# A two-layer trunk on one core: the last 16 tokens of the expert layer's first product by gathered rows, its dense part 240 columns wide

## The chip, the cores and the metric

The kernel runs on one core of a Trainium2 chip. The metric is the device time of one execution in microseconds (us), the median of several runs. Inside a core, TensorE (PE) multiplies matrices, VectorE (DVE), ScalarE (ACT) and GpSimd (POOL) work element by element, SyncE (SP) starts most of the transfers, and the DMA engines carry data between device memory and the core. Each engine works through its own list of instructions in order; they wait for one another by semaphores.

## What is computed

Two layers; each mixes tokens (`x + g1 * ...`) and then sends every token through a product-key retrieval over 16,384 one-neuron experts. With 256 tokens and a model width of 1024, the expert part is what the change touches:

```python
D_MODEL, SEQ, DEPTH = 1024, 256, 2
PEER_HEADS, PEER_TOPK, N_KEYS = 8, 16, 128

def peer_ffn(h, w_pq, sub_keys, expert_down, expert_up):
    ...
        q = (t @ w_pq).reshape(T, PEER_HEADS, 2, PEER_HALF)
        s = jnp.einsum('thpk,hpnk->thpn', q, sub_keys, preferred_element_type=jnp.float32)
        top_s, top_i = lax.top_k(s, PEER_TOPK)
        ...
        gate = jax.nn.softmax(best_s, axis=-1)
        u = expert_down[experts]
        act = jax.nn.gelu(jnp.einsum('td,thkd->thk', t, u, preferred_element_type=jnp.float32),
                          approximate=False)
        wgt = (gate * act).astype(t.dtype)
        vv = expert_up[experts]
        return jnp.einsum('thk,thkd->td', wgt, vv)

def hybrid_layer(x, c_act, ...):
    mod = (c_act @ w_ada + b_ada)[:, None, :]
    sh1, sc1, g1, sh2, sc2, g2 = jnp.split(mod, 6, axis=-1)
    h = rms_norm(x, norm1_g) * (1 + sc1) + sh1
    ...
    x = x + g1 * (merged @ w_out)
    h2 = rms_norm(x, norm2_g) * (1 + sc2) + sh2
    x = x + g2 * peer_ffn(h2, peer_wq, peer_sub_keys, peer_down, peer_up)
```

Every token picks 8 x 16 = 128 experts.

## The kernel before

A layer has these stages: a bridge that normalises the tokens, mixing (16 chunks of `w_in`, attention and its companions, 8 chunks of `w_out`), a second bridge, retrieval (16 chunks of `w_pq` and the two top-k searches, much of whose DVE work is put off as "fill"), the first product, the second product, and a closing combine.

**Weights.** A weight chunk is 128 x 1024 float32, 512 KB. SP loads it into one of seven `raw` buffers in the order of one long list (`seq`); ACT casts it to `hi` (L236), DVE takes the rest as `lo` (L229), each with three buffers. A chunk is then 24 matmuls in the one-pass type fp32r: for each of eight slices `d` of the model width hi times hi (L308), lo times hi (L309) and hi times lo (L310). The tokens `hh` are the moving operand, all 256 columns of them. Between weight chunks of `seq` stand "ada" chunks of `w_ada`: DVE multiplies one with the conditioning vector and sums it (L194) to get 128 entries of `mod`, needed by the next layer's bridges and gates. `mix` spreads them over a stretch of the list.

**First product.** The dense product of all tokens with all 128 chunks of `down` gives `ch`, 128 experts x 256 tokens per chunk; ACT applies the gelu. For the first `T` = 192 tokens the gates are spread over the expert grid by one-hot matrices: for each group of four tokens POOL compares an index row with `picks` four times (L925, f16), DVE compares (L928) and multiplies the result by the gates' two f16 parts (L930, twice 512 wide), and PE multiplies the two (L938, L939: eight f16 matmuls of 128 columns a group, 48 groups a layer). DVE multiplies gates and activations (L946 and the L97x lines). One-hots have two buffers (`R_ON`), so POOL and DVE build at most two groups ahead of PE. While fill work is left, `run_fill` works off a portion of it after every chunk; the gates start when the fill is empty. The last 64 tokens go another way: their activations are stored in device memory (`act_rows`), and the chosen ones, and the rows of `up`, are gathered by POOL with indirect DMAs (L1014, L1007).

**Second product.** 128 chunks of `up`, ten matmuls of 512 columns each (L1045), for the first 192 tokens; beside it DVE adds the gathered rows for the last 64 (L1041) by weights that L1032 to L1034 make. `R_ROWS` is where gathered rows land.

**What sets the order.** Each engine's list comes from a scheduler that simulates the program, except in the bridges and the combine, which are written out by hand. In the bridge DVE writes the normalised tokens slice by slice (L356, L428; ACT's part is L358), and PE follows with the first chunks' matmuls slice by slice (`second_pair`). The first two chunks of layer 1's `w_in` are used whole, in float32 (L388), and hold their `raw` buffers until then.

## Time and profile before

| | |
|---|---|
| median of 3 runs | 1744.12 us (1743.03 to 1744.75) |
| the profiled execution | 1742.29 us, of which the span is 1740.6 us |
| TensorE's granted clock, mean | 0.998 of full speed |

| stretch, us from the span's start | length | PE busy | DVE busy | POOL busy |
|---|---|---|---|---|
| first product, layer 0: 188.65 to 582.46 | 393.81 | 393.75 | 345.43 | 249.12 |
| second product, layer 0: 582.46 to 879.44 | 296.98 | 296.98 | 266.66 | 181.15 |
| first product, layer 1: 1039.40 to 1433.05 | 393.65 | 393.59 | 299.42 | 212.01 |
| second product, layer 1: 1433.05 to 1729.60 | 296.55 | 296.55 | 264.97 | 176.26 |

The busy time of an engine is the sum of its instructions' durations, overlaps counted once. PE's matmuls overlap: one of 287 ns starts some 119 ns after the one before. What counts for PE is therefore the distance between two starts.

### The profile page before, as it was taken

The numbers are of one execution on the slowest core, as the hardware profiler recorded it, in microseconds if no ns is written. First come the engines' busy times: TensorE is split into PE (matmuls) and PEld (weight loads), VectorE is DVE, ScalarE is ACT, GpSimd is POOL, SyncE is SP. The second block draws the span as 40 slices with busy tenths as digits, with TensorE's granted clock in tenths as the row PEclk, the third lists the DMA queues.
The fourth block names the chain that finished last, engine by engine and source line by source line (L and its number), as shares of the span: only waits on it lengthen the run. The fifth ranks groups of instructions, "written<-read, shape, count | busy, mean of one in ns | idle before, by whom it ended". The sixth has DMA issues, their size and how long they took to land.

```text
span 1740.6 us, 32293 instructions
## 1 busy us (share of the span) xinstructions
PE 1716.8 (99%) x11848; PEld 1573.4 (90%) x11848; DVE 1435.0 (82%) x2679; ACT 906.9 (52%) x1469; POOL 835.3 (48%) x697
## 2 busy tenths in 40 slices
PE   7999999999999999999999999999999999999998
PEld 6889999999999888888888999999999998888887
DVE  6858998888898799999966699957777768999996
ACT  2446455555444555555557555544544455555553
POOL 1000205588998477776100012236777737777630
PEclk9999999999999999999999999999999999999999
DMA  9965568887778799999843545676656668999993
GB/s 381 341 234 175 163 210 278 304 262 253 257 250 262 240 344 392 383 352 383 325 149 122 170 162 182 202 248 197 196 188 197 192 194 283 378 394 347 375 368 114
DMA packets 159281, 454.49 MB, mean 261 GB/s; under 512 B 50513, under 2 KB 50897, under 8 KB 157970
## 3 DMA queue, kind: packets, MB, share of 16 engines
q1 hardware_dynamic: 99936, 363.38, 60.3%
q0 software_dynamic: 23936, 80.50, 12.2%
q10 hardware_dynamic: 35250, 8.56, 2.2%
q8 instruction: 93, 1.52, 0.4%
q14 instruction: 66, 0.54, 0.1%
HBM read 440.75 MB, written 11.54 MB: 260 GB/s over the span
## 4 chain that ended last, share of the span: by engine, by line
PE 90%; DVE 7%; DMA 1%; ACT 1%; issue 0%; SPq 0%; DVEq 0%; ACTq 0%
PE acc L1045 34%; PE ch L308 15%; PE ch L309 14%; PE ch L310 14%; PE ch L306 3%; DVE lo L229 2%; PE g L938 1%; PE g L939 1%; PE ch L388 1%; DMA raw<-in_w_ada 1%; PE acc L308 1%; PE acc L310 1%; PE acc L309 1%; DVE arena L770 1%; DVE arena L771 1%; DVE arena L769 1%
## 5 line engine op out<-in xcount | busy, mean ns | idle before, releaser
L236 ACT CAST hi<-raw 128x1024 fp32r<-128x1024 f32 x554 | 582.0, 1051 | 624.0 <-PE ch L310 337.4
L229 DVE TENSOR_TENSOR lo<-raw,hi 128x1024 fp32r<-128x1024 f32 x554 | 675.6, 1224 | 179.8 <-ACT hi L236 169.1
L308 PE MATMUL ch<-hh,hi 128*128 128x256 f32 x2336 | 669.4, 287 | 0.0
L309 PE MATMUL ch<-hh,lo 128*128 128x256 f32 x2336 | 662.2, 284 | 0.1
L310 PE MATMUL ch<-hh,hi 128*128 128x256 f32 x2336 | 660.8, 283 | 0.0
L925 POOL TENSOR_SCALAR arena<-iota,picks 128x128 f16<-128x128 f16 x384 | 431.0, 1139 | 238.0 <-PE g L939 110.3
L309 PEld LDWEIGHTS ch<-hh,lo 128*128 128x128 f32 x2336 | 442.3, 189 | 0.7 <-DVE lo L229 0.5
L308 PEld LDWEIGHTS ch<-hh,hi 128*128 128x128 f32 x2336 | 442.1, 189 | 0.3 <-issue 0.3
L310 PEld LDWEIGHTS ch<-hh,hi 128*128 128x128 f32 x2336 | 442.2, 189 | 0.0
L1045 PE MATMUL acc<-hi,hh 128*128 128x512 f32 x1536 | 400.1, 395 | 0.0
L1045 PEld LDWEIGHTS acc<-hi,hh 128*128 128x128 f32 x1536 | 289.3, 188 | 67.3
L1045 PE MATMUL acc<-lo,hh 128*128 128x512 f32 x1024 | 280.9, 395 | 0.0
L1007 POOL DMA_INDIRECT arena<-in_up,arena x128 | 181.3, 1417 | 112.3 <-DVE arena L1041 77.5
L1045 PEld LDWEIGHTS acc<-lo,hh 128*128 128x128 f32 x1024 | 192.9, 188 | 44.9
L1014 POOL DMA_INDIRECT arena<-act_rows,arena x128 | 182.0, 1422 | 85.0 <-PE acc L1045 46.8
L1041 DVE SCALAR_TENSOR_TENSOR arena<-arena 128x1024 f32<-128x1024 f32 x126 | 162.1, 1286 | 0.0
L194 DVE SCALAR_TENSOR_TENSOR raw<-raw,arena 128x1024 f32<-128x1024 f32 x96 | 116.7, 1220 | 9.4 <-DMA raw<-in_w_ada 5.8
L930 DVE TENSOR_TENSOR arena<-arena,parts 128x512 f16<-128x512 f16 x192 | 77.0, 441 | 31.2 <-PE g L938 31.2
L784 POOL CAST arena<-arena 128x512 f16<-128x512 uint32 x32 | 29.2, 925 | 139.5 <-DVE arena L773 108.0
L748 POOL DMA_DIRECT2D arena<-in_keys x2 | 1.1, 562 | 170.2 <-issue 117.2
L949 ACT ACTIVATE arena<-g 128x344 f32<-128x344 f32 (+23 forms) x96 | 31.2, 325 | 73.6 <-DVE arena L946 72.5
L989 DVE TENSOR_TENSOR hh<-arena,hh 128x768 fp32r<-128x768 f32 (+1 forms) x66 | 61.6, 934 | 1.1 <-ACT hh L987 1.1
(232 smaller groups left out, 1610.1 us busy)
## 6 DMA issues: line engine op xcount, KB each, us to landing
raw<-in_down SPq DMA_DIRECT2D x256, 512.0 KB
raw<-in_up SPq DMA_DIRECT2D x256, 512.0 KB
raw<-in_w_ada SPq DMA_DIRECT2D x96, 512.0 KB
raw<-in_w_pq SPq DMA_DIRECT2D x32, 512.0 KB
raw<-in_w_in SPq DMA_DIRECT2D x26, 512.0 KB
raw<-in_w_out SPq DMA_DIRECT2D x16, 512.0 KB
act_rows<-ungated ACTq DMA_DIRECT2D x128, 64.0 KB
arena<-in_w_in SPq DMA_DIRECT2D x6, 512.0 KB
```

The costliest lines, as they stand in the source:

```text
L194: op = nc.vector.scalar_tensor_tensor(raw, raw, 1.0, cact, op0=OP.mult, op1=OP.mult, accum_out=mods[layer][:, col:col + 1])
L229: nc.vector.tensor_sub(lo, raw, hi.bitcast(F32))
L236: nc.scalar.copy(hi, raw)
L308: nc.tensor.matmul(dst, hi[:, cols], k[0], start=start, stop=False, **kw)
L309: nc.tensor.matmul(dst, lo[:, cols], k[0], start=False, stop=False, **kw)
L310: nc.tensor.matmul(dst, hi[:, cols], k[1], start=False, stop=stop, **kw)
L925: nc.gpsimd.tensor_scalar(oh[:, i, :], iota, picks[:, t:t + 1], None, op0=OP.is_equal)
L930: nc.vector.tensor_tensor(og[j], on, wide(1 + j), op=OP.mult)
L1007: nc.gpsimd.indirect_dma_start(out=R_ROWS[slots[k]], out_offset=None, in_=rows, in_offset=bass.IndirectOffsetOnAxis(ap=where_row[:, k:k + ...
L1014: nc.gpsimd.indirect_dma_start(out=R_ACTS[:, k % (2 * GROUP), :], out_offset=None, in_=act_rows[layer][:, :], in_offset=bass.IndirectOffse ...
L1041: nc.vector.scalar_tensor_tensor(R_SUM, v, w8[:, k:k + 1], R_SUM, op0=OP.mult, op1=OP.add)
L1045: nc.tensor.matmul(acc[piece], w, u[:, lo:hi], start=piece not in opened, stop=last, skip_group_check=True)
```

## The change

The first product's dense part takes the first `TD` = 240 tokens. For the last `TA` = 16 tokens the 128 chosen rows of `down` are gathered (`fetch_few`: POOL, 16 indirect DMAs of 128 rows a layer, four in flight in `R_ROWS`) and multiplied with the token's own input by DVE (`dot`, 16 of 128 x 1024 a layer). `own_inputs` prepares these inputs: 16 matmuls with the identity, two ACT copies, seven DMAs on SP's queue. `few_weights` makes gelu times gate of the sums and sends them to `w8a` by eight DMAs; `weights` adds them. `to_picks` sends eight more small DMAs. A new input, `down_rows`, is the table laid out by rows.

The gated one-hots of a group are made by one DVE operation, 1024 wide, where there were two of 512. For that, the two one-hots share a tile and interleave: `oh`, PE's stationary operand, was contiguous and now has a stride of two elements.

Sixteen ada chunks of layer 1 (groups 3 and 4) move in `seq` from layer 0's first product to layer 1's `w_in`. Two small regions change place.

```diff
+TA = 16
+TB = TS - TA
+TD = S - TA
+EIGHTHS = P // TA
+DOT_LAST = 104
...
-            body += tail
+            body = mix(body, ada(1, [3, 4]), 2) + tail
...
-            dn = mix(dn, ada(0, [5], "held") + ada(1, range(5), "held"), 24, 124)
+            dn = mix(dn, ada(0, [5], "held") + ada(1, range(3), "held"), 24, 124)
...
+                for e in range(EIGHTHS):
+                    nc.sync.dma_start(few[e * TA:(e + 1) * TA, :2], chosen[P - TA:, :, e * TA:(e + 1) * TA])
...
-                nc.gpsimd.tensor_scalar(oh[:, i, :], iota, picks[:, t:t + 1], None, op0=OP.is_equal)
...
-            for j in range(2):
-                nc.vector.tensor_tensor(og[j], on, wide(1 + j), op=OP.mult)
+                nc.gpsimd.tensor_scalar(oh[:, i // 2, :, i % 2], iota, picks[:, t:t + 1], None, op0=OP.is_equal)
...
+            nc.vector.tensor_tensor(gated, on[:, :, None].to_broadcast(shape), of[:, :, :, None].to_broadcast(shape),
+                                    op=OP.mult)
...
-                nc.tensor.matmul(dst, oh[:, i, :], og[0][:, i // 2, :, i % 2], start=True, stop=False)
-                nc.tensor.matmul(dst, oh[:, i, :], og[1][:, i // 2, :, i % 2], start=False, stop=True)
+                at = slice(None), i // 2, slice(None), i % 2
+                nc.tensor.matmul(dst, oh[at], og[0][at], start=True, stop=False)
+                nc.tensor.matmul(dst, oh[at], og[1][at], start=False, stop=True)
...
+        def own_inputs(pss):
+
+            for h, ps in enumerate(pss):
+                for c in range(4):
+                    dst = ps[:, c * P:(c + 1) * P]
+                    for k in range(2):
+                        nc.tensor.matmul(dst, hh[:, k, 4 * h + c, P:S], identr, start=k == 0, stop=k == 1)
+                nc.scalar.copy(own[P // 2:, h * 512:(h + 1) * 512], ps[P // 2:, :])
+            for e in range(EIGHTHS - 1):
+                nc.sync.dma_start(own[e * TA:(e + 1) * TA], own[P - TA:])
...
+        def fetch_few(k):
+            if k < TA:
+                nc.gpsimd.indirect_dma_start(
+                    out=R_ROWS[k % 4], out_offset=None, in_=rows_down,
+                    in_offset=bass.IndirectOffsetOnAxis(ap=few_row[:, k:k + 1].bitcast(U32), axis=0))
+
+        def dot(k):
+
+            v = R_ROWS[k % 4]
+            tc.keep_in_program_order(nc.vector.scalar_tensor_tensor(
+                v, v, 1.0, own, op0=OP.mult, op1=OP.mult, accum_out=few_w[:, k:k + 1]))
...
+                nc.vector.tensor_add(w, w, w8a[:, g * GROUP:(g + 1) * GROUP])
...
-            chunk_mm(ps[:, j * S:(j + 1) * S], next_chunk())
+            w = next_chunk()
+            for d in range(DC):
+                products(ps[:, j * TD:(j + 1) * TD], w, slice(d * P, (d + 1) * P),
+                         (hh[:, 0, d, :TD], hh[:, 1, d, :TD]), d == 0, d == DC - 1)
...
+            if start is not None and i == start + 2:
+                for k in range(4):
+                    fetch_few(k)
+            at = (start or 128) + 8
+            while at <= i and dotted < min(TA, -(-TA * (i + 1 - at) // (DOT_LAST - at))):
+                dot(dotted)
+                fetch_few(dotted + 4)
+                dotted += 1
+                if dotted == TA:
+                    few_weights()
```

The lines of the changed kernel are 10 to 50 higher than those before. Three places of the order follow.

POOL's list in layer 0's first product; L925 and L939 are the one-hots, L1007 fetches rows of `up`, L1043 rows of `down`. Before:

```order
L784 CAST arena<-arena 128x512 x16
L925 TENSOR_SCALAR arena<-iota,picks 128x128 x12
L1007 DMA arena<-in_up,arena 128x1024 x4
L925 TENSOR_SCALAR arena<-iota,picks 128x128 x180
L1014 DMA arena<-act_rows_102,arena 128x64 x16
```

After:

```order
L794 CAST arena<-arena 128x512 x16
L939 TENSOR_SCALAR arena<-iota,picks 128x128 x12
L1043 DMA arena<-in_down_rows,few 128x1024 x4
L939 TENSOR_SCALAR arena<-iota,picks 128x128 x20
L1043 DMA arena<-in_down_rows,few 128x1024
L939 TENSOR_SCALAR arena<-iota,picks 128x128 x4
L1043 DMA arena<-in_down_rows,few 128x1024
L939 TENSOR_SCALAR arena<-iota,picks 128x128 x8
```

The fetches of `up` rows that stood behind the first three groups have gone further down, and the fetches of `down` rows now stand singly between one-hots, every four to twelve of them; each but the first four waits for the dot that frees its rows.

DVE's list in layer 0's first product, some two thirds in: L229 and L239 are `lo`, L194 and L204 ada, L930 and L944 the gated one-hots, L928 and L941 the plain ones, L974/L946 and L991/L963 the use of the gates, L1050 a dot. Before:

```order
L194 SCALAR_TENSOR_TENSOR raw,mod_110<-raw,arena 128x1024
L928 TENSOR_TENSOR arena<-iota_87,parts 128x512 x2
L229 TENSOR_TENSOR lo<-raw,hi 128x1024
L974 TENSOR_TENSOR arena<-arena,gt 128x2x104
L930 TENSOR_TENSOR arena<-arena,parts 128x512 x2
L946 SCALAR_TENSOR_TENSOR arena<-arena,g 128x86x4
L229 TENSOR_TENSOR lo<-raw,hi 128x1024
L194 SCALAR_TENSOR_TENSOR raw,mod_110<-raw,arena 128x1024
L928 TENSOR_TENSOR arena<-iota_87,parts 128x512
```

After:

```order
L204 SCALAR_TENSOR_TENSOR raw,mod_114<-raw,arena 128x1024
L941 TENSOR_TENSOR arena<-iota_87,parts 128x2x256 x2
L239 TENSOR_TENSOR lo<-raw,hi 128x1024
L991 TENSOR_TENSOR arena<-arena,gt 128x2x104
L944 TENSOR_TENSOR arena<-arena,parts 128x1024
L963 SCALAR_TENSOR_TENSOR arena<-arena,g 128x86x4
L1050 SCALAR_TENSOR_TENSOR arena,few<-arena 128x1024
L239 TENSOR_TENSOR lo<-raw,hi 128x1024
L941 TENSOR_TENSOR arena<-iota_87,parts 128x2x256
```

Where an ada operation stood, every second or third time a dot stands now, and the pairs of L930 are single.

DVE's list in the bridge into layer 1: L340 and L350 update the tokens, L404 and L414 sum squares, L324 and L334 end the norm, L356/L428 and L366/L438 write the normalised slices that PE waits for. Before:

```order
L1107 COPY arena<-acc 128x512 x2
L340 SCALAR_TENSOR_TENSOR arena<-acc,mod_109,arena 128x256 x8
L229 TENSOR_TENSOR lo<-raw,hi 128x1024
L404 TENSOR_TENSOR arena<-arena 128x256 x3
L229 TENSOR_TENSOR lo<-raw,hi 128x1024
L404 TENSOR_TENSOR arena<-arena 128x256 x3
L324 RECIPROCAL rn<-rn 128x2
L356 SCALAR_TENSOR_TENSOR arena<-arena,mod_110,g 128x256 x2
L428 SCALAR_TENSOR_TENSOR hh<-arena,mod_110,hh 128x256
L356 SCALAR_TENSOR_TENSOR arena<-arena,mod_110,g 128x256
```

After:

```order
L350 SCALAR_TENSOR_TENSOR arena<-acc,mod_113,arena 128x256 x4
L414 TENSOR_TENSOR arena<-arena 128x256 x3
L204 SCALAR_TENSOR_TENSOR raw,mod_114<-raw,arena 128x1024
L239 TENSOR_TENSOR lo<-raw,hi 128x1024 x2
L414 TENSOR_TENSOR arena<-arena 128x256 x3
L204 SCALAR_TENSOR_TENSOR raw,mod_114<-raw,arena 128x1024
L334 RECIPROCAL rn<-rn 128x2
L366 SCALAR_TENSOR_TENSOR arena<-arena,mod_114,g 128x256 x2
L204 SCALAR_TENSOR_TENSOR raw,mod_114<-raw,arena 128x1024
L438 SCALAR_TENSOR_TENSOR hh<-arena,mod_114,hh 128x256
L366 SCALAR_TENSOR_TENSOR arena<-arena,mod_114,g 128x256
L438 SCALAR_TENSOR_TENSOR hh<-arena,mod_114,hh 128x256
```

Ada operations now stand in this bridge, nine of the sixteen ahead of its last slice; the sixth to the ninth stand behind the second group of sums, and three of those between the slices (after `L366 ... x2` and further on). The raw buffers of the seventh and eighth are those of the two whole chunks, which PE gives back after the last L388.

## Rows read from the trace of the kernel before

**Rows 1.** The page: busy time by engine, and the chain of work that ended last by engine and by line.

```profile
PE 1716.8 (99%) x11848; PEld 1573.4 (90%) x11848; DVE 1435.0 (82%) x2679; ACT 906.9 (52%) x1469; POOL 835.3 (48%) x697
...
PE 90%; DVE 7%; DMA 1%; ACT 1%; issue 0%; SPq 0%; DVEq 0%; ACTq 0%
PE acc L1045 34%; PE ch L308 15%; PE ch L309 14%; PE ch L310 14%; PE ch L306 3%; DVE lo L229 2%; PE g L938 1%; PE g L939 1%; PE ch L388 1%; DMA raw<-in_w_ada 1%; PE acc L308 1%; PE acc L310 1%; PE acc L309 1%; DVE arena L770 1%; DVE arena L771 1%; DVE arena L769 1%
```

**Rows 2.** The same chain in order of time, the two second products: start, length, what. A row is 1,278 records of 512 columns.

```profile
582.46 296.98 PE acc L1045 x1278
...
1433.05 296.52 PE acc L1045 x1276
```

**Rows 3.** Busy time by stretch, of the instructions on tile `ch` alone: 19 chunks of the fill part (the count has three records that reach in from outside); columns: stretch and length, PE, PEld, DVE, ACT, granted clock, DMA share, GB/s.

```profile
212.83:266.94 54.11, 54.11 (x459) 54.11 (x457) 0.00 (x0) 6.53 (x20) 1.00 0.66 205
```

**Rows 4.** PE in order of time in the gate part: a group's eight f16 matmuls of 128 columns, and fp32r matmuls behind it; start, duration.

```profile
453.11 0.22 PE L939 MATMUL g<-arena 128*128 128x128 f16 x1
...
453.45 0.22 PE L939 MATMUL g<-arena 128*128 128x128 f16 x1
...
453.92 0.29 PE L308 MATMUL ch<-hh,hi 128*128 128x256 f32 x1
...
455.12 0.29 PE L309 MATMUL ch<-hh,lo 128*128 128x256 f32 x1
```

**Rows 5.** The chain in order of time: float32 records of 128 columns (L628), and of 64 columns (L1116, the width is in rows 6).

```profile
83.50 0.89 PE g L628 x8
...
880.36 0.22 PE acc L1116 x2
```

**Rows 6.** PE in order of time: the operation of the last row above, whose records the timeline sets a little earlier than the chain.

```profile
880.20 0.39 PE L1116 MATMUL acc<-fold,arena 128*128 128x64 f32 x2
```

**Rows 7.** Groups of instructions by line: count, busy time, mean ns of one, idle time ahead and what ended it.

```profile
L925 POOL TENSOR_SCALAR arena<-iota,picks 128x128 f16<-128x128 f16 x384 | 431.0, 1139 | 238.0 <-PE g L939 110.3 <-DVE arena L838 52.5 <-DVE picks L855 52.0
L1007 POOL DMA_INDIRECT arena<-in_up,arena x128 | 181.3, 1417 | 112.3 <-DVE arena L1041 77.5 <-issue 14.2 <-DVE arena L1000 9.2
L1041 DVE SCALAR_TENSOR_TENSOR arena<-arena 128x1024 f32<-128x1024 f32 x126 | 162.1, 1286 | 0.0
L194 DVE SCALAR_TENSOR_TENSOR raw<-raw,arena 128x1024 f32<-128x1024 f32 x96 | 116.7, 1220 | 9.4 <-DMA raw<-in_w_ada 5.8 <-ACT arena L363 3.6
L930 DVE TENSOR_TENSOR arena<-arena,parts 128x512 f16<-128x512 f16 x192 | 77.0, 441 | 31.2 <-PE g L938 31.2
L938 PE MATMUL g<-arena 128*128 128x128 f16 x384 | 53.9, 222 | 0.0
L938 PEld LDWEIGHTS <-arena 128*128 128x128 f16 x384 | 35.2, 96 | 3.4
L308 PEld LDWEIGHTS ch<-hh,hi 128*128 128x128 f32 x2336 | 442.1, 189 | 0.3 <-issue 0.3
L824 DVE TENSOR_TENSOR arena<-arena,iota 128x2048 f16<-128x2048 f16 x8 | 9.7, 1212 | 0.0
L194 DVE DVE_READ_ACCUMULATOR raw<-raw,arena 128x1 f32 x96 | 8.1, 84 | 0.0
L336 ACT ACT_TABLE_LOAD x6 | 7.7, 1283 | 0.1
```

**Rows 8.** Busy time by stretch, all instructions: most of the fill part, then the gate part of layer 0 and of layer 1. Columns: length, PE, PEld, DVE, ACT, POOL, granted clock, DMA share, GB/s.

```profile
201.79:265.41 63.62, 63.62 (x539) 63.62 (x538) 63.59 (x241) 32.75 (x49) 5.12 (x5) 1.00 0.66 203
...
318.00:500.00 182.00, 182.00 (x1648) 180.77 (x1647) 156.12 (x280) 89.64 (x178) 156.31 (x133) 1.00 0.80 257
...
1170.00:1390.00 220.00, 220.00 (x1991) 218.52 (x1990) 160.76 (x281) 107.49 (x213) 164.94 (x164) 1.00 0.62 193
```

**Rows 9.** The bridge into layer 1, the chain in order of time: PE's last L388 and the norm's broadcast, then the first slice.

```profile
885.17 6.13 PE ch L388 x28
...
893.06 0.46 PE g L330 x4
893.55 0.49 DVE arena L356
894.06 0.52 ACT hh L358
```

**Rows 10.** DVE in order of time in the same bridge; idle time ahead in brackets.

```profile
882.25 0.69 DVE L1107 COPY arena<-acc 128x512 f32<-128x512 f32 x1 [2.78 <-PE acc L1045]
882.86 3.23 DVE L340 SCALAR_TENSOR_TENSOR arena<-acc,mod,arena 128x256 f32<-128x256 f32 x8
...
892.42 0.17 DVE L324 RECIPROCAL rn<-rn 128x2 f32<-128x2 f32 x1 [1.76 <-ACT rn L323]
893.55 0.87 DVE L356 SCALAR_TENSOR_TENSOR arena<-arena,mod,g 128x256 f32<-128x256 f32 x2 [0.96 <-PE g L330]
894.60 0.48 DVE L428 SCALAR_TENSOR_TENSOR hh<-arena,mod,hh 128x256 fp32r<-128x256 f32 x1 [0.18 <-ACT hh L358]
```

**Rows 11.** Busy time by stretch, columns as in rows 8: the bridge's end, layer 1's `w_in`, and ACT's fullest part of it.

```profile
888.00:896.00 8.00, 6.87 (x41) 5.93 (x39) 4.90 (x12) 3.79 (x10) 0.00 (x0) 1.00 0.70 223
900.00:945.00 45.00, 45.00 (x373) 43.99 (x373) 31.66 (x69) 32.65 (x76) 0.00 (x0) 1.00 0.43 141
928.00:936.00 8.00, 8.00 (x65) 7.58 (x64) 7.87 (x26) 7.32 (x31) 0.00 (x0) 1.00 0.41 132
```

More of the change, by code (lines that the diff above doesn't have):

```diff
@@ L57, in hybrid_trunk @@
 def hybrid_trunk(ctx: ExitStack, tc: tile.TileContext, x_in, c_in, vec_in, w_ada, w_in, w_out, w_pq,
-                 keys, down, up, rel_bias, sgu_w, sgu_b, out):
+                 keys, down, up, down_rows, rel_bias, sgu_w, sgu_b, out):
     nc = tc.nc
@@ L101, in hybrid_trunk @@
     c_dram = dram.tile([1, D], F32, name="c_dram")
-    act_rows = [dram.tile([P * P, TS], F32, name=f"act_rows{n}") for n in range(DEPTH)]
+    act_rows = [dram.tile([P * P, TB], F32, name=f"act_rows{n}") for n in range(DEPTH)]
     x_dram = dram.tile([P, DC * S], F32, name="x_dram")
@@ L143, in hybrid_trunk @@
     R_SUM = region(112 * S, D)
-    R_ACTS = region(116 * S, 2 * GROUP, TS)
-    R_IX = region(120 * S, 3, TS)
+    R_ACTS = region(116 * S, 2 * GROUP, TB)
+    own = region(120 * S, D)
     R_S = region(80 * S, 2, 16, P)
@@ L155, in hybrid_trunk @@
     R_SCR = region(116 * S, 2, 256)
+    chosen = region(108 * S, 2, P)
     R_PK = region(118 * S, 10, P)
@@ L991, in split @@
                     splits[i + k] = hi[:, k, :P], lo[:, k, :P], slot[:, k, T + P:2 * T + TS]
-        rows = up.rearrange("l j i c -> (l j i) c")
-        where_act, where_row, w8 = (R_IX[:, n, :] for n in range(3))
+        rows, rows_down = (w.rearrange("l j i c -> (l j i) c") for w in (up, down_rows))
+        where_act, where_row, w8, w8a = (index[:, n, :] for n in range(4))
+        few_at, few_gate, few_row, few_w = (few[:, n, :] for n in range(4))
         free = deque(range(4))
@@ L1134, in experts @@
         start = None
+        dotted = 0
         for i in range(128):
@@ L1152, in experts @@
                 start = i + 1
+                own_inputs([bank("acc", 4) for _ in range(2)])
                 make_onehots(0)
```

58 lines of the change are left out of this document (37 added, 21 removed).

## The prediction

> **What bounds the kernel now.** I read the shares of the page first: PE is busy for 99% of the span, and the chain that ended last runs over PE for 90% of it, mostly over the second product (L1045) and the first (L308 to L310) [rows 1]. So a change is worth what it takes from PE's list, as long as no other engine becomes late. The chain by time then shows both second products as one gapless piece each, 297 us [rows 2]; the change doesn't touch them. In the first product I read what one matmul takes. In the fill part 456 fp32r matmuls of 256 columns take 54.11 us, 118.7 ns each [rows 3]; in the gate part ten distances take 1.20 us, 120 ns each [rows 4]. Last, the stretches of the other engines: in the fill part DVE is busy for 63.59 of 63.62 us, in layer 0's gate part DVE and POOL both for 156 of 182 us, in layer 1's DVE for 161 and POOL for 165 of 220 us [rows 8]. There is little room in layer 0.
>
> **The narrower product.** It has 2 x 128 x 24 = 6144 matmuls. For the distance at 240 columns there is no row. From 256 to 512 columns it grows from 120 ns to 296.98/1278 = 232.4 ns [rows 2, 4], 0.44 ns a column, so 16 columns are worth 7.0 ns and 6144 matmuls 43.0 us. The upper bound is the shortest distance that any 4-byte record shows: 8 float32 records of 128 columns take 0.89 us, 111 ns each [rows 5], and with 64 columns it is no less, 0.22 us for two [rows 5, 6]. Half the columns and the same distance: there something else than the columns sets it, and loading weights is what they have in common. Down to 111.5 ns the gain is 8.5 ns a matmul, 52 us. The lower bound is nothing, if the distance at 256 columns is already set by weights. I take 43.0, by the slope, whose result of 113 ns lies just above the floor.
>
> The rows show that floor of 111 ns for 4-byte weights. The Trainium skill, "TensorE: Matmul & The Clock Gate", section "LDWEIGHTS (loading the stationary operand)", says that a load takes its column count over 1.2 ns, 107 ns for 128 columns, and the section "Back-to-back issue gap" gives a lone matmul N/2.4 + 2.5 ns, 109 ns for 256 columns. By these two the distance would go from 109 to 107 ns, an estimate of 2.5 ns or 15 us in place of 43. The traced 120 and 232 ns are 11 and 17 ns longer than that formula's, so I follow the slope; no run shown here has 240 columns.
>
> **Added to PE.** `own_inputs`: 32 matmuls of 128 columns at the floor's 111 ns, 3.6 us. They stand in bridges where PE partly waits for slices, so nothing to 3.6; I take 3.6.
>
> **The fill part.** DVE is full there now and makes 23 `lo` in 63.62 us, 2.77 us a chunk [rows 8]. PE would need 24 x 113 ns = 2.71 us. For some 25 chunks a layer DVE sets the pace: 2 x 25 x 0.06 = 3 us given back (0 to 5).
>
> **The gate part, layer 0.** Of the 182 us [rows 8], 1648 records less 266 f16 ones are fp32r: 1382 x 7.0 = 9.7 us go, leaving 172.3 us of PE. DVE: 33 groups lose two L930 of 441 ns and get one of 1024 columns; 441 ns for 512 and 1212 ns for 2048 [rows 7] give 0.70 us by interpolation, so -6.1 us. Of ada, 48 operations over the list's chunks 24 to 124 become 32, so 28 in these 58 chunks become some 19, of 1.22 + 0.08 us each: -12.1 us. Dots: 16 over the 70 chunks up to 104, 14 in this stretch, at L1041's 1286 + 84 ns, +19.2 us. DVE: 156.1 + 1.0 = 157.1 of 172.3 us, 91%: it fits. POOL gets 14 indirect DMAs at L1007's 1.417 us [rows 7], 156.3 + 19.8 = 176.1 us against 172.3. It doesn't fit, and every fetch but the first four waits on POOL's queue for a dot of DVE, with the next one-hots queued behind it and PE waiting for them two groups later. Now PE is ahead of POOL often enough: POOL waited 110 us for L939 [rows 7]. I take 3.8 us for the excess and about as much again for the waits: 8 us (0 to 16, the end where each of 16 fetches costs a DVE operation of a microsecond).
>
> **The gate part, layer 1.** POOL: 164.9 + 22.7 of 220 - 11.6 = 208.4 us, 90%, and DVE has room as well [rows 8]. Nothing, as long as POOL stays under PE.
>
> **Transfers.** The 16 gathered blocks a layer are as many bytes as 16 ada chunks, so layer 0's first product moves what it did, at a DMA share of 0.80 [rows 8]. SP's 23 small DMAs a layer stand between `raw` loads, each behind what it waits for; seven buffers hold 7 x 2.7 = 19 us of PE's work, so I cost them at nothing. A wait longer than that would reach PE with its excess.
>
> **The ada chunks moved.** They cost nothing in layer 0 and now sit in layer 1's bridge. Four come early, two of them around the copies and L340 on the path [rows 10], up to 2 x 1.3 us; two more hide before L324, where DVE idled 1.76 us and PE worked for 6.13 us on L388 [rows 9, 10]. The seventh to ninth stand between the slices for which PE waits: 3 x 1.3 = 3.9 us, straight on the path. The seventh's load also starts only after the last L388, at some 893 us; 0.52 MB at the 223 GB/s of that stretch [rows 11] is 2.4 us, where DVE would be there at 894.4 [rows 10], a wait of about 1 us. In `w_in` DVE has 31.66 of 45 us busy [rows 11] and gets seven more, 9 us: it fits, nearly. Two table loads of 1.28 us [rows 7] on ACT at 7.32 of 8 us [rows 11] and one more `hi` in the bridge: some 2 us. Together 9 us (3 to 14).
>
> **The sum.** 1742.3 (the profiled execution) - 43.0 + 3.6 + 3 + 8 + 9 = 1722.9 us. That execution lies 1.8 us below the median, so 1724.7, rounded 1725. With every cost at its upper bound it is 1740; with the floor and every cost at its lower bound 1695, but a PE that fast meets DVE and POOL sooner, so the forecast's own range ends at 1703.
>
> **The rivals.**
> *Strided weights, slower.* `oh` is loaded with a stride of two. Today eight f16 matmuls start 57 ns apart (0.34 us for six) [rows 4] and their loads are 96 ns records, against 189 for 4-byte weights [rows 7]: they load faster. If the stride ends that, 768 matmuls go from 58 to 111 ns, +41 us, and POOL's 8 us vanish behind it: 1758. It decides from about 83 ns on: 25 ns x 768 is the whole forecast gain. For it: the rate is visibly not the 4-byte one and nothing strided is in the trace. Against it: the operation stays f16 with 128 columns. The Trainium skill, same page, "Weight-path perf modes", says that the fast load takes packed or strided columns; by that, no cost, and no run here shows it.
> *Weights set the distance, slower.* If the 120 ns are the 111 of a 4-byte weight load and a fixed rest, 240 columns save nothing, DVE and POOL aren't pressed, and 3.6 + 9 us are added: 1744.1 + 12.6 = 1757. For it: 120 is near 111. Against it: the columns from 256 to 512 cost 0.44 ns each, so 256 lies on the slope or close to its foot. If the foot lies between 240 and 256 and a third of the gain is left, 14 us against 3.6 + 9 + 2, it is 1744, no change. The estimate of 15 us by the skill's two sections above would come out there.
> *POOL paces both gate parts.* If fetch, dot and one-hot chain up so that a group takes what it took, the 4944 matmuls outside the fill part lose all 34.6 us in place of 8: 1751. For it: POOL 102% in layer 0. Against it: 90% in layer 1, which is why I hold half of it, 1734, for part of the forecast.
> *Below 256 columns fp32r isn't one pass.* A float32 product shows at least two records a matmul of 111 ns and more [rows 5, 6]; twice the distance would add 0.7 ms or more. No row shows a narrower fp32r.
>
> **How the numbers follow.** Forecast 0.65 (1703 to 1741), deeper gain at the floor with all costs hidden 0.03, strided 0.10, weights 0.06, the third of the gain 0.06, POOL in both 0.08, more passes 0.02. Faster by over 0.2% (about what a measurement of this kernel can tell from no change; below 1740.6): 0.68. Same: 0.06. Slower: 0.26. Range 1703 to 1752, which takes in the forecast, the third of the gain and POOL in both: 0.79.
>
> **What would show it.** Right: `ch` matmuls 112 to 113 ns apart in both parts; DVE full in the fill part; POOL near full in layer 0's gate part with waits for dots ahead of fetches and PE waits for one-hots of some 8 us, none in layer 1; f16 matmuls still 58 ns apart; the bridge into layer 1 some 6 us longer with ada operations between slices. Wrong: 118 ns or more at 240 columns, 111 ns at L938's successor, or gate parts no shorter than before in both layers.

## The result, and the profile after

The changed kernel takes 1764.57 us (median of 4 runs, 1762.34 to 1765.57) beside 1743.84 us before (4 runs): ratio 1.0117, interval 1.0099 to 1.0134. It is slower by some 20 us where 19 us less were forecast, and outside the range. The span of the profiled execution is 1760.6 us.

The page after, busy time and the chain that ended last, to be read beside [rows 1]:

```profile
PE 1700.4 (97%) x11880; PEld 1543.2 (88%) x11880; DVE 1468.0 (83%) x2669; ACT 908.1 (52%) x1477; POOL 924.4 (53%) x729
...
PE 78%; DVE 11%; DMA 4%; POOL 3%; ACT 2%; issue 2%; SPq 0%; DVEq 0%; ACTq 0%; POOLq 0%
```

PE is busy 16 us less in a span that is 20 us longer: it waits where it did not wait before. POOL has come onto the chain, and DVE and DMA have more of it than before.

The stretches below are from the traces: the first product from its first `ch` matmul to the first matmul of the second product; "bridge and mixing" from the start of the last matmul of L1045's kind in layer 0 to the first fp32r matmul on `ch` of layer 1's retrieval. (e1's expectation counts the latter from the end of the second product's gapless piece, some 3 us earlier: 140.6 us after the change.) "All else" is the rest of the span. Each row is one profiled execution, and runs of one kernel lie 1 to 7 us apart, so a difference of two or three us between rows isn't shown by them. The experiments' kernels are described further down.

| us | first product, layer 0 | bridge and mixing, layer 1 | first product, layer 1 | all else | span |
|---|---|---|---|---|---|
| before | 393.7 | 117.2 | 393.5 | 836.2 | 1740.6 |
| the change | 399.6 | 137.7 | 384.7 | 838.6 | 1760.6 |
| ada back (e1) | 412.4 | 118.4 | 384.1 | 841.2 | 1756.1 |
| no gather, no dots (e2) | 374.5 | 139.2 | 372.0 | 839.1 | 1724.8 |
| dense 256 (e3) | 406.7 | 138.0 | 398.7 | 838.5 | 1781.9 |
| before, ada moved (e4) | 394.0 | 136.8 | 394.0 | 838.4 | 1763.2 |
| fetches alone (e5) | 389.6 | 138.8 | 382.9 | 838.4 | 1749.7 |
| dots alone (e6) | 389.6 | 138.0 | 375.7 | 838.7 | 1742.0 |
| ada held (e7) | 400.8 | 131.0 | 386.3 | 842.0 | 1760.1 |
| a third of the one-hots on DVE (e8) | 378.1 | 138.2 | 375.9 | 838.5 | 1730.7 |
| all one-hots on DVE (e9) | 373.1 | 138.5 | 372.0 | 838.3 | 1721.9 |
| e9 with ada back (e10) | 378.3 | 118.4 | 371.8 | 839.3 | 1707.8 |
| no gather, 224 columns (e11) | 374.3 | 138.4 | 371.6 | 839.5 | 1723.8 |
| short ada operations (e12) | 401.9 | 126.6 | 384.3 | 840.8 | 1753.6 |

**The narrow matmul does what was forecast.** Busy time by stretch, of the instructions on `ch` alone, seven chunks of the fill part (columns as in [rows 3]):

```profile
247.41:266.17 18.76, 18.76 (x171) 18.76 (x169) 0.00 (x0) 2.49 (x8) 1.00 0.69 217
```

168 matmuls in 18.76 us are 111.7 ns each, where [rows 3] have 118.7 (three of the 171 records reach in from outside). In these seven chunks of 2.68 us PE has no gap. Earlier in the fill part it has: four chunks take 2.88 to 3.48 us, and there PE is late at the matmul that needs `lo`. Its two longest waits, idle time in brackets:

```profile
216.70 0.38 PE L319 MATMUL ch<-hh,lo 128*128 128x240 f32 x1 [0.53 <-DVE lo L239]
...
234.01 0.38 PE L319 MATMUL ch<-hh,lo 128*128 128x240 f32 x1 [0.50 <-DVE lo L239]
```

The four chunks are 2.0 us longer than four of PE's own pace, and the same four in layer 1 too. Before the change all of them took 2.85 us, like their neighbours.

**The gate part stalls.** Groups by line, the columns of [rows 7]:

```profile
L939 POOL TENSOR_SCALAR arena<-iota,picks 128x128 f16<-128x128 f16 x384 | 475.7, 1284 | 142.7 <-DVE picks L871 105.4 <-PE g L956 36.1
...
L955 PE MATMUL g<-arena 128*128 128x128 f16 x384 | 60.0, 223 | 24.2 <-POOL arena L939 24.0
...
L1043 POOL DMA_INDIRECT arena<-in_down_rows,few x32 | 44.0, 1374 | 25.1 <-DMA raw<-in_down 12.0 <-DVE few L1039 8.2 <-issue 1.8
```

POOL's one-hots take 1284 ns on average, 1139 before, and POOL's own wait for PE has fallen from 110 to 36 us [rows 7]. PE now waits 24 us for POOL ahead of L955, the f16 matmuls (L938 before, 0.0 us), in 44 places. The fetches (L1043) take POOL 1.37 us each. Of the 25.1 us ahead of them 12.0 and 8.2 are single waits, each ahead of a layer's first fetch; the other thirty have 5 us between them, so they found their dots done. One place where PE waits, POOL in order of time (between the last two rows stand four more one-hots):

```profile
398.92 1.56 POOL L1043 DMA_INDIRECT arena<-in_down_rows,few  x1
400.52 2.10 POOL L939 TENSOR_SCALAR arena<-iota,picks 128x128 f16<-128x128 f16 x1
402.57 1.88 POOL L939 TENSOR_SCALAR arena<-iota,picks 128x128 f16<-128x128 f16 x1
404.40 2.55 POOL L939 TENSOR_SCALAR arena<-iota,picks 128x128 f16<-128x128 f16 x1
406.90 0.63 POOL L939 TENSOR_SCALAR arena<-iota,picks 128x128 f16<-128x128 f16 x1
...
410.41 1.01 POOL L1043 DMA_INDIRECT arena<-in_down_rows,few  x1
```

and all engines beside it (columns as in [rows 8]):

```profile
400.52:406.90 6.38, 5.45 (x51) 5.24 (x49) 6.16 (x10) 3.45 (x7) 6.38 (x3) 1.00 0.92 322
...
409.06:410.27 1.21, 0.58 (x4) 0.23 (x4) 0.00 (x0) 0.36 (x1) 1.21 (x3) 1.00 0.86 323
```

The same instruction takes 1.9 to 2.6 us while DVE is busy for 6.16 of 6.38 us, with a dot, two `lo` and an ada operation among it, and 0.63 us where DVE has run dry. It is so throughout: of the 384 one-hots the 36 with no DVE instruction beside them take 0.63 to 0.67 us, and the 209 beside which DVE is busy for over nine tenths take 1.55 us on average. PE there, with its idle time in brackets:

```profile
399.75 0.22 PE L956 MATMUL g<-arena 128*128 128x128 f16 x1
...
400.09 0.22 PE L956 MATMUL g<-arena 128*128 128x128 f16 x1
...
407.01 0.23 PE L955 MATMUL g<-arena 128*128 128x128 f16 x1 [1.04 <-POOL arena L939]
...
409.16 0.23 PE L955 MATMUL g<-arena 128*128 128x128 f16 x1 [0.70 <-POOL arena L939]
...
410.33 0.29 PE L955 MATMUL g<-arena 128*128 128x128 f16 x1 [0.30 <-POOL arena L939]
...
410.83 0.41 PE L319 MATMUL ch<-hh,lo 128*128 128x240 f32 x1
411.05 0.41 PE L320 MATMUL ch<-hh,hi 128*128 128x240 f32 x1
```

At 399.75 a group runs as it did in [rows 4], six distances in 0.34 us: the strided weights cost nothing. At 407 PE waits for one-hot after one-hot, and POOL has been busy since 398.9. Behind the stall the fp32r matmuls are 0.21 us apart instead of 0.11. The granted clock, by stretch (columns as in [rows 8]):

```profile
407.00:410.40 3.40, 1.51 (x11) 0.65 (x12) 1.06 (x2) 0.36 (x1) 3.27 (x5) 0.98 0.80 274
410.40:414.60 4.20, 4.20 (x25) 4.20 (x26) 3.83 (x7) 0.36 (x1) 4.15 (x3) 0.61 0.58 178
414.60:420.00 5.40, 5.40 (x55) 5.37 (x53) 3.88 (x7) 3.04 (x6) 5.40 (x7) 1.00 0.58 184
```

PE was busy for 1.51 of 3.40 us, and in the next 4.2 us the mean granted clock is 0.61: for most of them the matmuls run at the lower of the two levels, 1.2 GHz. So this stall costs its own length and then some. But most stalls don't do this. In the two first products the clock falls at four places only:

```profile
368.00:374.00 6.00, 5.41 (x34) 5.24 (x35) 4.05 (x7) 0.44 (x1) 6.00 (x7) 0.72 0.49 164
409.00:415.00 6.00, 5.24 (x32) 4.90 (x33) 4.24 (x8) 0.74 (x3) 5.83 (x7) 0.72 0.65 217
487.00:493.00 6.00, 4.98 (x30) 4.46 (x31) 3.28 (x6) 0.28 (x1) 5.83 (x8) 0.72 0.87 287
1320.00:1326.00 6.00, 5.24 (x32) 4.90 (x33) 3.03 (x6) 0.63 (x2) 5.83 (x9) 0.72 0.81 269
```

In all the rest of these two stretches it is 1.00.

**The bridge into layer 1 is longer.** DVE in order of time, beside [rows 10]:

```profile
904.59 1.22 DVE L204 SCALAR_TENSOR_TENSOR raw<-raw,arena 128x1024 f32<-128x1024 f32 x1 [2.48 <-DMA raw<-in_w_ada]
...
905.74 0.16 DVE L334 RECIPROCAL rn<-rn 128x2 f32<-128x2 f32 x1
907.22 0.87 DVE L366 SCALAR_TENSOR_TENSOR arena<-arena,mod,g 128x256 f32<-128x256 f32 x2 [1.32 <-PE g L340]
908.37 1.23 DVE L204 SCALAR_TENSOR_TENSOR raw<-raw,arena 128x1024 f32<-128x1024 f32 x1 [0.28 <-DMA raw<-in_w_ada]
...
911.57 1.23 DVE L204 SCALAR_TENSOR_TENSOR raw<-raw,arena 128x1024 f32<-128x1024 f32 x1 [0.38 <-DMA raw<-in_w_ada]
```

DVE stands before an ada operation whose chunk hasn't landed, and behind it stands L334, whose result PE needs: 2.48 us, where the prediction had let this operation hide. In the whole stretch the view of waits has

```profile
DVE raw L204 <- DMA raw<-in_w_ada: 12.0, 11, 2.5
```

(us in all, times, longest). Five of the eleven waits, 6.1 us, lie before the end of the bridge. PE waits for DVE, and its clock falls here too, which it did not before (columns as in [rows 8]):

```profile
896.00:904.00 8.00, 5.77 (x26) 4.98 (x25) 5.04 (x9) 3.78 (x8) 0.00 (x0) 0.86 0.51 167
904.00:912.00 8.00, 5.58 (x19) 4.08 (x19) 5.43 (x12) 1.93 (x5) 0.00 (x0) 0.50 0.83 295
```

### The profile page after: what moved, and what is told of

The parts are those of the page before. It is cut to its first block, busy times and chain, and to the rows that moved or that the text cites. A ratio compares the mean times of both kernels' runs of the same rounds, so it can differ in the third digit from the quotient of the medians.

```text
span 1760.6 us, 32503 instructions
## 1 busy us (share of the span) xinstructions
PE 1700.4 (97%) x11880; PEld 1543.2 (88%) x11880; DVE 1468.0 (83%) x2669; ACT 908.1 (52%) x1477; POOL 924.4 (53%) x729
## 4 chain that ended last, share of the span: by engine, by line
PE 78%; DVE 11%; DMA 4%; POOL 3%; ACT 2%; issue 2%; SPq 0%; DVEq 0%; ACTq 0%; POOLq 0%
PE acc L1095 34%; PE ch L318 11%; PE ch L319 11%; PE ch L320 11%; POOL arena L939 3%; DVE lo L239 3%; PE ch L316 3%; DMA raw<-in_w_ada 2%; PE g L955 1%; DMA raw<-in_down 1%; PE g L956 1%; DVE arena L781 1%; PE ch L398 1%; DVE arena L783 1%; DVE arena L780 1%
## 5 line engine op out<-in xcount | busy, mean ns | idle before, releaser
L239 DVE TENSOR_TENSOR lo<-raw,hi 128x1024 fp32r<-128x1024 f32 x554 | 677.1, 1228 | 131.7 <-ACT hi L246 122.8
L318 PE MATMUL ch<-hh,hi 128*128 128x240 f32 (+1 forms) x2336 | 653.9, 280 | 0.5 <-ACT hi L246 0.5
L319 PE MATMUL ch<-hh,lo 128*128 128x240 f32 (+1 forms) x2336 | 649.1, 278 | 2.8 <-DVE lo L239 2.6
L320 PE MATMUL ch<-hh,hi 128*128 128x240 f32 (+1 forms) x2336 | 646.5, 277 | 0.0
L939 POOL TENSOR_SCALAR arena<-iota,picks 128x128 f16<-128x128 f16 x384 | 475.7, 1284 | 142.7 <-DVE picks L871 105.4
L1063 POOL DMA_INDIRECT arena<-act_rows,index x128 | 186.8, 1459 | 82.0 <-PE acc L1095 43.9
L1025 POOL DMA_INDIRECT arena<-in_up,index x128 | 177.7, 1388 | 99.1 <-DVE arena L1091 76.3
L1091 DVE SCALAR_TENSOR_TENSOR arena<-arena,index 128x1024 f32<-128x1024 f32 x126 | 162.1, 1286 | 1.5 <-DVE lo L239 0.8
L204 DVE SCALAR_TENSOR_TENSOR raw<-raw,arena 128x1024 f32<-128x1024 f32 x96 | 117.0, 1224 | 22.3 <-DMA raw<-in_w_ada 18.4
L944 DVE TENSOR_TENSOR arena<-arena,parts 128x1024 f16<-128x1024 f16 x96 | 69.7, 727 | 45.1 <-PE g L956 45.1
L955 PE MATMUL g<-arena 128*128 128x128 f16 x384 | 60.0, 223 | 24.2 <-POOL arena L939 24.0
```

The lines of the kernel that those rows point to most:

```text
L204: op = nc.vector.scalar_tensor_tensor(raw, raw, 1.0, cact, op0=OP.mult, op1=OP.mult, accum_out=mods[layer][:, col:col + 1])
L239: nc.vector.tensor_sub(lo, raw, hi.bitcast(F32))
L318: nc.tensor.matmul(dst, hi[:, cols], k[0], start=start, stop=False, **kw)
L319: nc.tensor.matmul(dst, lo[:, cols], k[0], start=False, stop=False, **kw)
L320: nc.tensor.matmul(dst, hi[:, cols], k[1], start=False, stop=stop, **kw)
L939: nc.gpsimd.tensor_scalar(oh[:, i // 2, :, i % 2], iota, picks[:, t:t + 1], None, op0=OP.is_equal)
```

## The experiments

Three things were to be told apart: what the gathers and dots cost, and through which engine; what the moved ada chunks cost, and where; and whether the narrow product and the one-hots' new form do what was taken for them. Times are medians; ratios are to the kernel before, run on the same chip. The scheduler orders the lists anew for every edit, so more than the edited lines can move: in e5 the last fetch of layer 0 starts at 357 us, in the change at 470.

**e1, the ada chunks back in layer 0.**

```diff
-            body = mix(body, ada(1, [3, 4]), 2) + tail
+            body += tail
...
-ada(1, range(3), "held"), 24, 124)
+ada(1, range(5), "held"), 24, 124)
```

> The changed kernel with its sixteen ada chunks back in layer 0's first product. Theory 'ada in the bridge' (most of the 21 us by which layer 1's bridge and mixing became longer come from DVE waiting there, in order, for the loads of moved ada chunks): that stretch, from the end of layer 0's second product to the first chunk of layer 1's retrieval, falls from 140.6 to about 120 us; layer 0's gate part has 16 more DVE operations of 1.3 us and gets longer by 0 to 12 us; in all 1744 to 1757 us. Rival 'own inputs' (the extra matmuls, copies and table loads make that stretch longer): the stretch stays over 135 us, in all 1760 us or more.

1758.20 us, ratio 1.0078 (1.0061 to 1.0094), 1 us above the theory's range. Bridge and mixing fall by 19.3 us to 118.4, within 1.2 us of before: the ada chunks are that cost, and own inputs and table loads are not. Layer 0's first product grows by 12.8 us, just over the upper end of 12, where sixteen operations of 1.3 us come on top of a POOL that is late already.

**e2, without gathers and dots.** The loop that calls `dot`, `fetch_few` and `few_weights` is taken out.

> The changed kernel without the gathers of down rows, the dots and their weights; it leaves out the first product of the last 16 tokens. Theory 'POOL paces' (PE's stalls in the gate parts come from the fetches on POOL's queue and from dots that slow POOL): PE waits for one-hots fall from 24 us to under 3, layer 0's first product becomes some 25 us and layer 1's some 13 us shorter, in all 1722 to 1732 us. Rival 'one-hot form' (the 1024-wide operation or the interleaved one-hots slow POOL or PE): the stalls stay, over 1750 us.

1726.11 us, ratio 0.9892 (0.9876 to 0.9909). The first products shrink to 374.5 and 372.0 us, 25.1 and 12.7 us below the change, and PE's wait for POOL falls from 24 to 1.6 us. With the same 1024-wide operation and the same strided weights nearly all stalls are gone: the one-hots' form is not their main cause. It does take a little of POOL's slack: with no DVE instruction beside it a one-hot took 0.60 us before and takes 0.63 to 0.64 us in the change and here, some 14 us over all 384. Against the kernel before it is 19.2 and 21.5 us a layer, which is what the narrow product is worth without gathers and dots.

**e3, dense product 256 wide.**

```diff
-                products(ps[:, j * TD:(j + 1) * TD], w, slice(d * P, (d + 1) * P),
-                         (hh[:, 0, d, :TD], hh[:, 1, d, :TD]), d == 0, d == DC - 1)
+                products(ps[:, j * S:(j + 1) * S], w, slice(d * P, (d + 1) * P),
+                         (hh[:, 0, d, :S], hh[:, 1, d, :S]), d == 0, d == DC - 1)
```

The gelus that read the chunk get the wider view too.

> The changed kernel with the dense product 256 columns wide again, all the rest of the change kept (the last 16 columns are computed and not used). Theory 'the narrow product saves, POOL takes part of it back': chunks in the fill part go from 2.68 to 2.85 us, POOL's stalls shrink, since PE gives it 0.2 us a chunk more; 43 us less some 15 to 24 us: 1783 to 1793 us. Rival 'POOL paces everything outside the fill part': only 50 chunks x 0.17 us and the like come back, 1773 to 1778 us. Rival 'width does nothing': 1765 us.

1785.29 us, ratio 1.0233 (1.0216 to 1.0250). So width is worth some 21 us under the change's own stalls (spans of 1781.9 and 1760.6), half of 43, as the first theory had it: PE's wait for POOL falls from 24 to 11 us because a slower PE gives POOL more time.

**e4, the kernel before with the ada chunks moved.** The first line of e1's diff the other way round, in the kernel before, and `range(3)` for `range(5)`.

> The kernel before with one part of the change, the sixteen ada chunks moved to layer 1's w_in. Theory 'ada in the bridge': layer 1's bridge and mixing get 15 to 21 us longer and layer 0's first product, where PE has no gap, stays as it was: 1759 to 1765 us. Rival 'own inputs': the move costs little by itself, 1744 to 1750 us.

1765.73 us, ratio 1.0121 (1.0104 to 1.0138), 1 us above the theory's range. Bridge and mixing 136.8 us, layer 0's first product unchanged. One part of the change alone, with none of the others, makes the kernel as slow as the whole change.

**e5, fetches alone.**

```diff
-                dot(dotted)
                 fetch_few(dotted + 4)
                 dotted += 1
-                if dotted == TA:
-                    few_weights()
```

> The changed kernel with its 32 gathers of down rows but without the dots and their weights (leaves out the first product of the last 16 tokens). Without either, POOL waited 83 us for PE in the two gate parts; the fetches take 32 x 1.4 = 44 us of that. Theory 'sum of both' (POOL loses its slack only to fetches and to one-hots slowed by dots together): the stalls mostly vanish, 1727 to 1742 us. Rival 'the fetch alone' (its place in POOL's queue ahead of one-hots stalls PE, whatever DVE does): 1750 to 1765 us.

1753.72 us, ratio 1.0058 (1.0042 to 1.0075): in the rival's range. The first products are 15.1 and 10.9 us longer than in e2.

**e6, dots alone.** `fetch_few` is not called, and a dot reads `own` twice.

> The changed kernel with its 32 dots but without the gathers: each dot multiplies the token's input with itself in place of a gathered row, so that the first product of the last 16 tokens is not what it should be. Theory 'sum of both': dots make one-hots some 80 ns slower, 31 us of POOL's slack of 83 us, and the stalls mostly vanish, 1727 to 1740 us. Rival 'the dot alone' (DVE gets too full or blocks POOL): 1750 to 1765 us.

1746.17 us (10 runs), ratio 1.0014 (1.0005 to 1.0024): between the two ranges. The first products are 15.1 and 3.7 us longer than in e2. POOL's one-hots take 1333 ns on average here; in e2 they take 1202 and in e5, fetches without dots, 1165:

```profile
L939 POOL TENSOR_SCALAR arena<-iota,picks 128x128 f16<-128x128 f16 x384 | 492.8, 1333 | 175.3 <-PE g L956 69.6 <-DVE arena L848 52.7 <-DVE picks L871 52.6
```

DVE slows POOL. So the theory that only both together use up POOL's slack fell: POOL's slack of 83 us in e2 is an average, and either part alone stalls PE for 10 to 12 us although 52 to 70 us of POOL's waits for PE remain.

**e7, ada chunks held behind a `lo`.**

```diff
-            body = mix(body, ada(1, [3, 4]), 2) + tail
+            body = mix(body + tail, ada(1, [3, 4], "held"), 6, 22)
```

> The changed kernel with the moved ada chunks still in layer 1's mixing, but behind w_in chunk 6 up to the middle of w_out, each DVE operation placed right after a lo: none stands in the bridge. Theory 'waits in the bridge' (what costs is that DVE waits in order for late loads ahead of the slices that PE needs, and what follows from it): the stretch from layer 0's second product to layer 1's retrieval falls from 138 to 118 to 125 us, in all 1745 to 1753 us. Rival 'too much work' (sixteen more loads and DVE operations in that stretch cost the same wherever they stand): 132 us or more, 1758 us or more.

1757.83 us, ratio 1.0073 (1.0056 to 1.0090). Bridge and mixing 131.0 us, between both ranges. The bridge is as it was before: the first slice's matmul comes 12.8 us after the stretch's start (before 12.8, the change 18.2), the first matmul on `ch` behind the bridge after 19.3 us (19.3, 28.8). But the rest of the stretch takes 111.7 us where it took 97.9 before and 108.9 in the change. Of the 20.5 us, then, 9.5 are the bridge's, and they go when nothing stands in it; with the operations moved out of it the rest gets no better (2.8 us longer in this execution, which is the slowest of the four runs): half of both theories.

**e12, the ada operations shortened.** The sixteen operations work on 8 columns, at the same places.

```diff
+        n = 8 if layer == 1 and 24 <= col < 40 else D
-        op = nc.vector.scalar_tensor_tensor(raw, raw, 1.0, cact, op0=OP.mult, op1=OP.mult,
+        op = nc.vector.scalar_tensor_tensor(raw[:, :n], raw[:, :n], 1.0, cact[:, :n], op0=OP.mult, op1=OP.mult,
```

> The changed kernel with the sixteen moved ada operations cut to 8 of their 1024 columns, at the same places of DVE's list and with the same loads (leaves out nearly all of those 128-entry sums). Theory 'waits for loads' (what the move costs in layer 1's bridge and mixing is that DVE waits in order for chunks that land late, and PE for DVE): that stretch stays at 130 to 138 us, against 117 before the change, in all 1756 to 1765 us. Rival 'the work' (16 x 1.2 us of DVE are on the path): it falls to 118 to 125 us, in all 1744 to 1752 us.

1753.72 us, ratio 1.0052 (1.0035 to 1.0068), between the two ranges. Bridge and mixing 126.6 us, between them too: 11.1 of the 20.5 us go with DVE's work, 9.4 stay without it. In the bridge nearly all stays: 27.2 us to the first `ch` matmul, 28.8 with the work. An operation of 0.17 us still holds DVE up for its chunk:

```profile
908.22 0.17 DVE L205 SCALAR_TENSOR_TENSOR raw<-raw,arena 128x8 f32<-128x8 f32 x1 [2.81 <-DMA raw<-in_w_ada]
...
913.41 0.17 DVE L205 SCALAR_TENSOR_TENSOR raw<-raw,arena 128x8 f32<-128x8 f32 x1 [2.20 <-DMA raw<-in_w_ada]
```

In the whole stretch these waits even grow:

```profile
DVE raw L205 <- DMA raw<-in_w_ada: 19.8, 8, 4.9
```

19.8 us here, 12.0 in the change, and yet the stretch is 11 us shorter, so the sum of the waits doesn't measure what they cost. In the bridge it is the waits for loads, and behind the bridge mostly the work. Neither theory holds for the whole.

**e8, a third of the plain one-hots on DVE.**

```diff
-                nc.gpsimd.tensor_scalar(oh[:, i // 2, :, i % 2], iota, picks[:, t:t + 1], None, op0=OP.is_equal)
+                eng = nc.vector if g % 3 == 2 else nc.gpsimd
+                eng.tensor_scalar(oh[:, i // 2, :, i % 2], iota, picks[:, t:t + 1], None, op0=OP.is_equal)
```

> The changed kernel with every third group's plain one-hots (the four that POOL compares) made by DVE instead. Theory 'POOL paces the gate parts': POOL has 128 one-hots less, 160 us, PE's waits for POOL nearly vanish, layer 0's first product falls from 400 to 378 to 385 us and layer 1's from 385 to 373 to 377 us, in all 1728 to 1740 us. Rival 'DVE paces them' (POOL is slow because DVE is full, and DVE gets fuller): 1755 us or more.

1731.92 us, ratio 0.9931 (0.9914 to 0.9947), faster than before. DVE gets 31.2 us more work in all, and the stretches shrink to 378.1 and 375.9 us. So what held up the gate parts was POOL and not a full DVE.

**e9, all one-hots on DVE.** `picks` becomes a second f16 row of `parts`, and one comparison makes both one-hots of a group.

```diff
-            oh, on = both[:, :, 0], both[:, :, 1]
-            for i in range(4):
-                t = 4 * g + i
-                nc.gpsimd.tensor_scalar(oh[:, i // 2, :, i % 2], iota, picks[:, t:t + 1], None, op0=OP.is_equal)
+            oh, on = both[:, :, 1], both[:, :, 0]
...
-            nc.vector.tensor_tensor(on, iota2[:, None, :, :].to_broadcast([P, 2, P, 2]),
-                                    which[:, :, 0][:, :, None, :].to_broadcast([P, 2, P, 2]), op=OP.is_equal)
             shape = [P, 2, 2, P, 2]
+            nc.vector.tensor_tensor(both, iota2[:, None, None].to_broadcast(shape),
+                                    which[:, :, :, None].to_broadcast(shape), op=OP.is_equal)
```

> The changed kernel with all one-hots made by DVE: one comparison 1024 wide makes the plain one-hots of both sides of a group, where DVE made 512 and POOL four times 128. POOL keeps only the fetches. Theory 'POOL paces the gate parts': no PE wait for one-hots is left, DVE has some 0.3 us more a group, 14 us a layer; layer 0's first product 374 to 382 us, layer 1's 371 to 376 us, in all 1724 to 1734 us. Rival 'the gathers cost by themselves' (dots on DVE or the rows' transfers delay PE without POOL): 390 us in layer 0, over 1742 us.

1725.22 us, ratio 0.9904 (0.9888 to 0.9921). With all gathers and all dots the first products take 373.1 and 372.0 us, no more than in e2 without them:

```profile
L939 DVE TENSOR_TENSOR arena<-iota,parts 128x1024 f16<-128x1024 f16 x96 | 65.8, 687 | 19.4 <-PE g L953 17.8 <-issue 0.9 <-PE ch L320 0.5
...
L1040 POOL DMA_INDIRECT arena<-in_down_rows,few x32 | 49.5, 1548 | 410.9 <-DVE arena L1047 246.9 <-PE ch L320 162.1 <-issue 1.5
```

96 operations of 687 ns on DVE replace 384 of 1284 ns on POOL and the comparisons of 512 that DVE made already. The fetches now wait for the dots at leisure, and nobody waits for them.

**e10, the same with the ada chunks back.** e9 and e1's diff.

> The same with the sixteen ada chunks back in layer 0's first product. Theory: layer 1's bridge and mixing fall by 19 us to 118 us, as they did with the ada chunks back before; layer 0's first product pays only what DVE lacks, 0 to 8 us and not the 13 us that it paid with POOL in the way: 1706 to 1718 us. Rival 'DVE is the next bound in layer 0' (its 16 operations of 1.3 us all come on top): layer 0's first product over 390 us, 1725 us or more.

1709.68 us, ratio 0.9806 (0.9790 to 0.9822): the best version, 1.9% below the kernel before. Bridge and mixing are back at 118.4 us, and layer 0's first product pays 5.2 us for the sixteen operations, in place of the 12.8 in e1. From 80 us into it on DVE is nearly full there, busy for 280.94 of 298.34 us (columns as in [rows 8]):

```profile
270.46:568.80 298.34, 294.65 (x2778) 291.67 (x2777) 280.94 (x437) 150.68 (x302) 30.30 (x20) 1.00 0.90 305
```

**e11, 224 columns.** e2 with `TA = 32`.

> The changed kernel without gathers and dots, with a dense product of 224 columns in place of 240 (leaves out the first product of the last 32 tokens); to be read against the run without gathers at 240. Theory 'floor' (weights set the 111.7 ns at 240 columns): the distance of ch matmuls stays at 111 to 112 ns, the time within 5 us of 1726 us. Rival 'slope' (0.44 ns a column goes on): 104 to 105 ns, some 35 to 43 us less where DVE and POOL can follow, 1690 to 1715 us.

1726.01 us, ratio 0.9901 (0.9884 to 0.9917), e2's time. The same seven chunks:

```profile
248.28:267.04 18.76, 18.76 (x171) 18.76 (x169) 0.00 (x0) 2.38 (x8) 1.00 0.69 210
```

111.7 ns again: 240 columns stand at the floor already, and 224 buy nothing more.

## Why the prediction was wrong

**The narrower product** was right in its mechanism. 43.0 us were forecast; without gathers and dots 40.7 came (e2: 19.2 + 21.5, with own inputs outside these stretches and with what the fill part loses inside). The floor of 111 ns of [rows 5] is real and was met (e11), so the rival of weights that set the distance at 256 columns already is refuted. So is that of strided weights, by the distances in the trace after, and that of more passes.

**Own inputs** were forecast at 3.6 us and cost 2.4. In each layer sixteen of their matmuls stand among the first two fp32r chunks of the retrieval, which take 7.74 us with them and 6.54 before; that is the 1.2 us by which e1's bridge and mixing are longer. One adds 75 ns, not the 111 of the sum: matmuls in a row of equals meet that floor (the change, e11), a single one among wider ones does not. **The fill part** was forecast at 3 us and cost 4: DVE did hold PE up, as forecast, though in four chunks a layer and not in all.

**The gate parts** are the first failed step. "I take 3.8 us for the excess and about as much again for the waits: 8 us" and, for layer 1, "Nothing, as long as POOL stays under PE" were 25.1 and 12.7 us (the change less e2). The cause was named rightly, POOL, and e8 and e9 show it: with the one-hots on another engine and all gathers kept the cost is gone. Three things made the size wrong. The sum took one-hots at their old duration and only added the fetches; but a busy DVE slows them, from 0.63 to some 2 us in the rows above, and with the dots their mean is 1333 ns (e6) and 1284 ns (the change) against 1202 in e2 and 1139 before. It compared means over 182 us; but a fetch stands between the one-hots of two groups, POOL is two groups ahead at most, and a lead lost there becomes a stall, whatever slack comes later: in layer 1, at a forecast 90%, it cost 12.7 us, and with fetches alone PE still stalled while POOL kept 52 us of waits for PE (e5). And at four places the granted clock fell behind a stall, which no term held. What the forecast took for half of its 8 us, fetches that wait for dots with the one-hots queued behind them, did not happen: the rows of L1043 have next to no such waits.

The gate part of layer 1 shows how little a mean says (columns as in [rows 8]):

```profile
1170.00:1390.00 220.00, 213.16 (x1989) 209.08 (x1988) 170.35 (x259) 109.38 (x217) 193.38 (x163) 0.99 0.73 241
```

POOL is busy for 88% of it, less than forecast, and PE idles for 6.8 us. The rival "POOL paces both gate parts", given 0.08, comes nearest in size (34.6 us for 37.8) but not in form: its group that takes what it took isn't there. Beside e2 nearly all of the 37.8 us lies in some 15 of layer 0's 128 chunks and 10 of layer 1's, and the others take as long as in e2.

Where the 37.8 us went can be read from PE. Against e2 it is idle for 23.1 us more in the two first products (27.0 and 3.9). The four places of 6.00 us at a mean clock of 0.72 lose 4 x 6.00 x 0.28 = 6.7 us, an estimate. The remaining 8 us are, as far as the rows show, matmuls that no longer overlap: a pair of f16 matmuls that waits for its one-hot keeps PE busy for 0.29 us, in an undisturbed group two distances of 57 ns, and there were 44 such waits.

The Trainium skill bears on the first of the three, the one-hots' duration. They take 0.63 us beside an idle DVE and 1.9 to 2.6 us beside a full one, and dots raise their mean from 1202 to 1333 ns. "SBUF — State Buffer", section "SBUF: two separate sides", says that VectorE, in an operation with two inputs from the core's memory, and GpSimd, when it reads there, take a shared port pair in turn, each for its whole instruction. A dot, `lo` and an ada operation have two such inputs, and these rows agree; no run here isolates a port. By the rule each of 32 dots of 1.22 us can hold POOL up for its length, 39 us at most, an estimate; e6's one-hots are 50 us longer in all than e2's, so the dots' own length does not account for all of it. The prediction should have used it.

**The ada chunks moved** are the second failed step: 9 us forecast, 19.3 measured (e1), 19.6 in e4. The places were the right ones: ada operations between the slices, DVE in order, loads that start late. The forecast let two more "hide before L324", and there DVE waited 2.48 us for a chunk; it priced one wait for a load at 1 us, and there were five up to the bridge's end, 6.1 us in all; PE's clock fell to 0.50 meanwhile. That gives 9.5 us in the bridge in place of some 7.5: ahead of the first slice 5.4 us came where 2.6 were forecast, among the slices 4.1 where 4.9 were. And "It fits, nearly" for `w_in` was worth another 10 us behind the bridge (11.0 less the 1.2 of own inputs), 1 or 2 forecast. e12 and e7 show that the bridge's part is the waits and the later part mostly the work.

The sum after the fact, from the table: -40.7 (narrow product, with the fill part's loss in it) + 37.8 (gathers and dots) + 20.5 (bridge and mixing) + 2.4 (all else, 1.2 of it own inputs) = +20.0 us, the difference of the two spans.

What stays open: how fetches and dots share the 37.8 us, since alone they cost 26.0 and 18.8, which overlap, and in e5 the fetches stand elsewhere; how much of what slows the one-hots is the shared port; what of the 9.5 us in the bridge is DVE's waiting and what the lower clock; and whether some order of the ada chunks in layer 1 costs less than e7.

## What to carry to other kernels

An engine that is busy for 90% of a long stretch can still hold up the engine that it feeds: count how far ahead it may run, and take each inserted instruction, with what it slows, against that lead and not against the mean. An operation moved to another place of an engine's in-order list brings its wait for data along; ahead of work on the path its data has to be there already. And a change that loses as a whole can pay once the engine in its way is relieved: the same gathers and dots that cost 38 us cost nothing after the one-hots had moved to DVE.
